# Four first column tiles woven together by halves of rows, and 512-column matmuls that take both halves of an activation in the last three projections

## The chip, the cores and the metric

One Trainium2 chip, one core of it. The metric is device microseconds (us) of one execution of the whole program. Engines are called PE (TensorE), DVE (VectorE), ACT (ScalarE), POOL (GpSimd) and SP (SyncE, which here only issues DMAs).

## The reference

One decoder layer over 16 learned meta tokens and 256 real tokens (T = 272 columns of work), width 2048. In short:

```
u     = rmsnorm(h, ln1_w)
p     = u @ w_in                       # one wide input projection for three mixers and three gates
o_h, o_m, o_r = hgrn2(p_h), mamba2(p_m), rwkv7(p_r)
mixed = g0 * (o_h @ w_up_h) + g1 * (o_m @ w_up_m) + g2 * (o_r @ w_up_r)
h     = h + mixed @ w_out
u     = rmsnorm(h, ln2_w)
h     = h + square(relu(u @ w_mlp_in)) @ w_mlp_out
return rmsnorm(h, lnf_w)               # the 256 real tokens
```

Everything is float32. The output projection is 2048 x 2048, the MLP 2048 x 8192 and 8192 x 2048.

## The kernel before

Tokens lie along the free axis and channels on the 128 partitions. Every projection is done one **column tile** at a time: 128 output channels, whose weights come as one or two **pieces** of 8 row blocks (128 x 1024 values, 512 KB each). `weights` (L210) has SP load a piece into `raw`, then calls `split` (L200): ACT rounds it to `wh` (fp32r, the high part), DVE subtracts and leaves the rest in `wl`. `raw`, `wh` and `wl` have three buffers each (`raw` gets three more after the output projection). Activations are split the same way, into `uh`/`ul` for the normed input, `mh`/`ml` for `mixed`, `zh`/`zl` for the second normed input and `hh`/`hl` for the hidden layer.

`product` (L228) then does three matmuls per row block into one of three PSUM buffers `pt`: high weights by high activations (L237), high weights by low activations (L238), low weights by high activations (L239). A full tile of 2048 rows is 16 row blocks, so 48 matmuls, each with its own weight load.

The program's stages are in this order: x is loaded and scaled (L276 to L285), its squares are summed on ACT, POOL, DVE and PE (L288 to L295), which gives `rstd1`; the RWKV tiles `wl`, `aldt`, `gl` 0 and `gl` 1 are projected one after the other (L365 to L375), each multiplied by `rstd1` in `proj` (L299); then come the other mixer tiles between the mixers' own small matmuls, the gates, and the three up-projections. Behind them stand the output projection (`out`, 16 tiles, L1161), and the MLP in four quarters: 16 tiles `mi` (2048 rows each, L1181) that fill a quarter of the hidden layer, then 16 tiles `mo` (L1190) that add it up in `macc`. The tail (L1205 to L1216) sums squares, takes the inverse root and scales the 16 output blocks on DVE and POOL, two blocks to a DMA.

Instructions are put in order for each engine by a scheduler that runs over the program with its own model of times; `tc.high_priority()` lets weight loads and splits go ahead. So the order on an engine isn't the order of the code, and a matmul that would wait for an activation can be put behind matmuls of the next tile.

Of the kernel before, what the change touches and what calls it, by code (L numbers as in the profile page):

```python
# [18 lines left out]
P = 128  # L19
D = 2048  # L20
# [130 lines left out]
def tile_hybrid(ctx: ExitStack, tc: tile.TileContext, a, out, dbg=None):  # L151
# [23 lines left out]
    def V(k, j=0, n=1, rows=slice(0, P)):  # L175
        return vecs[rows, VCOL[k] + j:VCOL[k] + j + n]
# [13 lines left out]
    def uname(s):  # L190
        cnt[0] += 1
        return f"{s}_{cnt[0]}"

    def trunk_psum(w):
        return ps_t.tile([P, 512], F32, tag="t", bufs=3, name=uname("pt"))[:, :w]

    def mx():
        return ps_x.tile([P, 512], F32, tag="x", bufs=5, name=uname("px"))

    def split(dst_h, dst_l, src):  # L200
        act.copy(dst_h, src)  # L201
        vec.tensor_tensor(dst_l, src, dst_h.bitcast(F32), sub)  # L202
# [69 lines left out]
    with ExitStack() as st:  # L272
        np_ = pool(st, "norm1", side="right")
        xt = np_.tile([P, KT, T], F32, name="xt")
        with tc.high_priority():
# [6 lines left out]
        for q in range(4):  # L282
            for kt in range(4 * q, 4 * q + 4):
                act.activation(uh[:, kt], xt[:, kt], AF.Copy, scale=V("ln1", kt))
                vec.scalar_tensor_tensor(ul[:, kt], xt[:, kt], V("ln1", kt),  # L285
                                         uh[:, kt].bitcast(F32), mult, sub)
        for q in range(4):
            x4 = xt[:, 4 * q:4 * q + 4]  # L288
            sq = np_.tile([P, 4, T], F32, tag="sq", bufs=2, name=uname("sq"))
            act.activation(sq[:, 0:2], x4[:, 0:2], AF.Square)  # L290
            nc.gpsimd.tensor_tensor(sq[:, 2:4], x4[:, 2:4], x4[:, 2:4], mult)
            nc.gpsimd.tensor_tensor(sq[:, 0:2], sq[:, 0:2], sq[:, 2:4], add)
            vec.tensor_tensor(sq[:, 0], sq[:, 0], sq[:, 1], add)
            pe.matmul(ssq, lhsT=C("ones"), rhs=sq[:, 0], start=(q == 0), stop=(q == 3))
        inv_sqrt(rstd1, ssq, 1.0 / D, eps_n)  # L295

    ALL, REAL = slice(0, T), slice(NM, T)

    def proj(key, tok=ALL, ahead=True):  # L299
        ps = product(key, uh, ul, tok, ahead=ahead)  # L300
        vec.tensor_tensor(ps, ps, rstd1[:, tok], mult)
        return ps


    omu = const.tile([P, 28], F32, name="omu")
    vec.tensor_scalar(omu, V("mu", 0, 28), -1.0, 1.0, mult, add)
    omka = const.tile([P, 8], F32, name="omka")
# [49 lines left out]
    REAL2 = slice(NM - 2, T)  # L357
# [6 lines left out]
    ps = proj("wl", ahead=False)  # L364
    shifted(ps, 24, twl[R96], R96)  # L365
    sigmoid(twl[R96], twl[R96], sign=2.0)
    vec.tensor_scalar(twl[R96], twl[R96], 2.0, -1.0, mult, add)
    ps = proj("aldt", ahead=False)
    shifted(ps, 25, alr[0:112], slice(0, 112))
    for j in range(2):  # L370
        ps = proj(("gl", j), REAL2)
        if j == 0:
            nc.sync.dma_start(cst, a["cst"])
        shifted(ps, 26 + j, sgl[:, j], skip=2)
        sigmoid(sgl[:, j], sgl[:, j])  # L375

    cr = {}
# [746 lines left out]
            nc.sync.dma_start(dbg[n], t)  # L1124
    st_x = ExitStack()
    xp = pool(st_x, "xp", side="right")
    mh = xp.tile([P, 16, NR], F32R, name="mh")
    ml = xp.tile([P, 16, NR], F32R, name="ml")
    hi, lo = branch_parts(o_h)
    for c in range(16):  # L1130
        up_next("uph", c, hi, lo, gate_back("gh", c))
        split(mh[:, c], ml[:, c], mixed[:, c])
    if "mixed" in dbg:
        nc.sync.dma_start(dbg["mixed"], mixed)
    st_g.close()
# [5 lines left out]
    ep = pool(st_e, "ep")  # L1141
    wp2 = pool(st_e, "wp2")
    h1 = ep.tile([P, 16, NR], F32, name="h1")
    zh = ep.tile([P, 16, NR], F32R, name="zh")
    zl = ep.tile([P, 16, NR], F32R, name="zl")
# [15 lines left out]
    for c in range(16):  # L1161
        xr = et("xr", 3)
        nc.scalar.dma_start(xr, a["xt"][:, c, NM:])
        ps = product(("out", c), mh, ml, RT)
        vec.tensor_tensor(h1[:, c], ps, xr, add)
        z = et("z")
        act.activation(z, h1[:, c], AF.Copy, scale=V("ln2", c))
        split(zh[:, c], zl[:, c], z)
        add_square(c, h1[:, c])
    more_raw.append((wp2, 3))  # L1170
    st_x.close()
# [5 lines left out]
    st_y = ExitStack()  # L1177
    yp = pool(st_y, "yp", side="right")
    for qd in range(4):
        hh = yp.tile([P, 16, NR], F32R, tag="hh", bufs=2, name=uname("hh"))  # L1180
        hl = yp.tile([P, 16, NR], F32R, tag="hl", bufs=2, name=uname("hl"))  # L1181
        for c in range(16):
            ps = product(("mi", 16 * qd + c), zh, zl, RT)
            r = et("rl")
            act.activation(r, ps, AF.Relu)
            s = et("rs")
            vec.tensor_tensor(s, r, r, mult)
            split(hh[:, c], hl[:, c], s)
# [21 lines left out]
    rf = et("rl")  # L1210
    inv_sqrt(rf, pn, 1.0 / D, eps_n)
    act.activation(h1[:, 15], h1[:, 15], AF.Copy, scale=V("lnf", 15))
    for c in range(16):
        (nc.gpsimd if c % 4 == 3 else vec).tensor_tensor(macc[:, c], h1[:, c], rf, mult)  # L1214
        if c % 2:
            (nc.sync if c % 4 == 1 else nc.scalar).dma_start(out[:, c - 1:c + 1], macc[:, c - 1:c + 1])  # L1216
    st_y.close()
    st_e.close()

# [95 lines left out]
```

## Time and profile before

| | |
|---|---|
| median of 3 runs | 1935.28 us (1934.91 to 1935.75) |
| the profiled execution, whole | 1936.93 us |
| its span, first to last instruction | 1935.1 us |
| PE busy | 1906.0 us of the span, 16220 matmuls |
| DVE, ACT, POOL busy | 1242.9, 1048.3, 185.5 us |
| HBM | 340 MB moved, 175 GB/s over the span |

The rows are those of one profiled execution. A matmul's listed time is from its start to the end of its result; a matmul starts long before the one ahead has ended, so the distance from one start to the next is what it costs, and the listed time is longer. The profile counts a plain float32 matmul as two (two passes), an fp32r matmul as one.

### The profile page before, as it was taken

To read this page: it belongs to the slowest core of one execution; us is meant where nothing else is said; L and a number is where in the kernel's file an instruction comes from. 1 tells how busy PE (TensorE), PEld (TensorE's weight loads), DVE (VectorE), ACT (ScalarE), POOL (GpSimd) and SP (SyncE) were. 2 spreads that over 40 slices of the span, in tenths; PEclk is the share of its full clock that TensorE was granted. 3 is DMA by queue.
4 is the path that set the end of the run, shared out by engine and by line. 5 is a ranking of instruction groups with operands and counts; after the bars stand their busy time and mean duration, and the time that the engine had idled before them with its cause. 6 is when DMAs were issued, how large, how long until landed. Compare 5 with 4: busy or idle time off the path is not lost.

```text
span 1935.1 us, 39773 instructions
## 1 busy us (share of the span) xinstructions
PE 1906.0 (98%) x16220; PEld 1866.0 (96%) x16220; DVE 1242.9 (64%) x1992; ACT 1048.3 (54%) x1857; POOL 185.5 (10%) x318
## 2 busy tenths in 40 slices
PE   6999999999999999999999999999999999999997
PEld 6999999999999999999999999999999999999997
DVE  7878676567956566777677765544455555665565
ACT  5666666566556667766564455444444344334453
POOL 4020111111111111112111000000000000000000
PEclk9999999999999999999999999999999999999999
DMA  5556544445554445445656776555555555555552
GB/s 211 183 179 202 164 150 135 146 154 158 175 174 147 145 144 193 144 150 168 200 168 213 247 218 190 182 184 185 185 186 185 186 183 181 185 185 183 185 185 99
DMA packets 104119, 340.39 MB, mean 176 GB/s; under 512 B 18216, under 2 KB 21432, under 8 KB 103936
## 3 DMA queue, kind: packets, MB, share of 16 engines
q1 hardware_dynamic: 91904, 315.25, 51.0%
q0 software_dynamic: 8576, 17.67, 3.0%
q10 hardware_dynamic: 3456, 4.93, 0.7%
q8 instruction: 127, 2.08, 0.5%
q14 instruction: 56, 0.46, 0.1%
HBM read 327.72 MB, written 10.08 MB: 175 GB/s over the span
## 4 chain that ended last, share of the span: by engine, by line
PE 97%; DVE 1%; DMA 0%; issue 0%; ACT 0%; SPq 0%; DVEq 0%; POOLq 0%
PE pt L239 29%; PE pt L237 29%; PE pt L238 29%; PE px L1025 1%; PE px L551 1%; PE px L657 0%; PE px L639 0%; PE px L694 0%; PE px L565 0%; PE px L559 0%; DVE macc L1214 0%; PE px L480 0%; PE px L623 0%; PE px L627 0%; PE px L661 0%; PE px L848 0%
## 5 line engine op out<-in xcount | busy, mean ns | idle before, releaser
L202 DVE TENSOR_TENSOR wl<-raw,wh 128x1024 fp32r<-128x1024 f32 x592 | 725.6, 1226 | 452.1 <-ACT wh L201 444.8
L201 ACT CAST wh<-raw 128x1024 fp32r<-128x1024 f32 x592 | 620.4, 1049 | 706.2 <-PE pt L238 491.1
L237 PE MATMUL pt<-uh,wh 128*128 128x256 f32 (+3 forms) x2048 | 587.6, 287 | 9.2 <-ACT wh L201 9.2
L239 PE MATMUL pt<-uh,wl 128*128 128x256 f32 (+3 forms) x2048 | 587.9, 287 | 4.0 <-DVE wl L202 4.0
L238 PE MATMUL pt<-ul,wh 128*128 128x256 f32 (+3 forms) x2048 | 587.6, 287 | 1.7 <-DVE ul L285 1.7
L237 PEld LDWEIGHTS pt<-uh,wh 128*128 128x128 f32 x2048 | 387.8, 189 | 12.6 <-ACT wh L201 9.2
L239 PEld LDWEIGHTS pt<-uh,wl 128*128 128x128 f32 x2048 | 387.7, 189 | 8.1 <-DVE wl L202 4.6
L238 PEld LDWEIGHTS pt<-ul,wh 128*128 128x128 f32 x2048 | 387.2, 189 | 6.3 <-DVE ul L285 2.6
L239 PE MATMUL pt<-zh,wl 128*128 128x256 f32 x1024 | 290.0, 283 | 0.0
L238 PE MATMUL pt<-zl,wh 128*128 128x256 f32 x1024 | 289.8, 283 | 0.0
L237 PE MATMUL pt<-zh,wh 128*128 128x256 f32 x1024 | 289.8, 283 | 0.0
L239 PE MATMUL pt<-hh,wl 128*128 128x256 f32 x1024 | 288.0, 281 | 0.0
L238 PE MATMUL pt<-hl,wh 128*128 128x256 f32 x1024 | 288.0, 281 | 0.0
L237 PE MATMUL pt<-hh,wh 128*128 128x256 f32 x1024 | 287.8, 281 | 0.0
L237 PEld LDWEIGHTS pt<-zh,wh 128*128 128x128 f32 x1024 | 196.6, 192 | 0.0
L239 PEld LDWEIGHTS pt<-zh,wl 128*128 128x128 f32 x1024 | 196.6, 192 | 0.0
L238 PEld LDWEIGHTS pt<-zl,wh 128*128 128x128 f32 x1024 | 196.6, 192 | 0.0
L237 PEld LDWEIGHTS pt<-hh,wh 128*128 128x128 f32 x1024 | 192.8, 188 | 0.0
L238 PEld LDWEIGHTS pt<-hl,wh 128*128 128x128 f32 x1024 | 192.7, 188 | 0.0
L239 PEld LDWEIGHTS pt<-hh,wl 128*128 128x128 f32 x1024 | 192.7, 188 | 0.0
L239 PE MATMUL pt<-oh,wl 128*128 128x256 f32 x384 | 108.3, 282 | 0.0
L237 PE MATMUL pt<-oh,wh 128*128 128x256 f32 x384 | 108.2, 282 | 0.0
(451 smaller groups left out, 2388.0 us busy)
## 6 DMA issues: line engine op xcount, KB each, us to landing
raw<-in_w SPq DMA_DIRECT2D x592, 512.0 KB, 3.5
rcb<-sc_rc SPq DMA_DIRECT2D x8, 256.0 KB, 4.1
sc_gr<-gt POOLq DMA_DIRECT2D x16, 128.0 KB, 3.7
sc_gm<-gt POOLq DMA_DIRECT2D x16, 128.0 KB, 3.6
sc_gh<-gt POOLq DMA_DIRECT2D x16, 128.0 KB, 3.7
gin<-sc_gr POOLq DMA_DIRECT2D x16, 128.0 KB, 3.0
gin<-sc_gm POOLq DMA_DIRECT2D x16, 128.0 KB, 3.1
gin<-sc_gh POOLq DMA_DIRECT2D x16, 128.0 KB, 3.4
```

The lines of the kernel that those rows point to most:

```text
L201: act.copy(dst_h, src)
L202: vec.tensor_tensor(dst_l, src, dst_h.bitcast(F32), sub)
L237: pe.matmul(ps, lhsT=wh[:, j], rhs=hi[:, kt, tok], start=(kt == 0), stop=False)
L238: pe.matmul(ps, lhsT=wh[:, j], rhs=lo[:, kt, tok], start=False, stop=False)
L239: pe.matmul(ps, lhsT=wl[:, j], rhs=hi[:, kt, tok], start=False, stop=(k == last and j == 7))
L551: pe.matmul(pk[e][:, c], lhsT=kt_[er, t], rhs=ar[er, :, t], start=True, stop=True)
L1025: pe.matmul(px[br, 2 * i + c], lhsT=xc, rhs=xc, start=True, stop=True)
```

## The change

At the start, all of x and the first three weight pieces are issued on SP's queue, in the order in which they are used. The tiles `wl`, `aldt`, `gl` 0 and `gl` 1 get a PSUM buffer each and are worked in two rounds: first the upper 8 row blocks of all four, then the lower 8. The splits of x (`x_parts`) stand between the splits of the first pieces. The squares and small preparations on DVE are told to come behind the last split of x, the sums of the squares go to POOL alone, and one matmul in place of four adds them over partitions.

In `out`, `mi` and `mo` the high and low activations lie in one tile (`m2`, `z2`, `hx`). `product2` does two matmuls per row block: high weights by 512 columns (both parts), whose results stand in the two halves of one PSUM bank, and low weights by the 256 high columns, added to the lower half. The two halves are added afterwards on DVE, where one of them must first be copied out by ACT (`low_part`) or goes through `h1` or `macc`.

In the tail the inverse root is written to PSUM and to SBUF; DVE scales 13 blocks in five instructions, POOL three, and six DMAs write the output.

```
+    def product2(key, x):
+        full = trunk_psum(2 * NR)
+        for k, (wh, wl) in enumerate(weights(key)):
+            for j in range(8):
+                kt = 8 * k + j
+                end = kt == KT - 1
+                pe.matmul(full.rearrange("p (a n) -> p a n", a=2), lhsT=wh[:, j], rhs=x[:, :, kt],
+                          start=(kt == 0), stop=end, skip_group_check=True)
+                pe.matmul(full[:, :NR], lhsT=wl[:, j], rhs=x[:, 0, kt], start=False, stop=end,
+                          skip_group_check=True)
+        return full[:, :NR], full[:, NR:]
...
+        FIRST = (("wl", ALL), ("aldt", ALL), (("gl", 0), REAL2), (("gl", 1), REAL2))
...
-            for q in range(4):
-                (nc.scalar if q else nc.sync).dma_start(xt[:, 4 * q:4 * q + 4],
-                                                        a["xt"][:, 4 * q:4 * q + 4])
+            load_x(0, 2)
+            raws = [raw_piece(FIRST[0][0], 0, 2)]
+            load_x(2, 4)
+            load_x(4, 8)
+            raws += [raw_piece(key, 0) for key, _ in FIRST[1:3]]
+            load_x(8, 12)
+            load_x(12, 16)
+        first = [mx()[:, :tok.stop - tok.start] for _, tok in FIRST]
...
+        for k in range(2):
+            for i, (key, tok) in enumerate(FIRST):
+                raw = raws.pop(0) if raws else raw_piece(key, k)
...
+                steps = 2 if k == 0 and i == 0 else 1
+                for m in range(steps):
+                    s = slice(8 // steps * m, 8 // steps * (m + 1))
+                    if steps == 2:
+                        x_parts(4 * m, 4 * m + 2)
+                    with tc.high_priority():
+                        split(wh[:, s], wl[:, s], raw[:, s])
+                    if steps == 2:
+                        x_parts(4 * m + 2, 4 * m + 4)
...
+                if k == 0 and i in (1, 2):
+                    x_parts(4 * i + 4, 4 * i + 8)
+        for q in range(8):
+            sq = np_.tile([P, 2, T], F32, tag="sq", bufs=2, name=uname("sq"))
+            with tc.issue_after(last_x[0]):
+                act.activation(sq if q else ssum, xt[:, 2 * q:2 * q + 2], AF.Square)
+            if q:
+                nc.gpsimd.tensor_tensor(ssum, ssum, sq, add)
+        nc.gpsimd.tensor_tensor(ssum[:, 0], ssum[:, 0], ssum[:, 1], add)
+        pe.matmul(ssq, lhsT=C("ones"), rhs=ssum[:, 0], start=True, stop=True)
...
+    def low_part(lo):
+        t = et("lo", 2)
+        act.copy(t, lo)
+        return t
...
-        ps = product(("out", c), mh, ml, RT)
-        vec.tensor_tensor(h1[:, c], ps, xr, add)
+        ps, lo = product2(("out", c), m2)
+        vec.tensor_tensor(h1[:, c], lo, xr, add)
+        vec.tensor_tensor(h1[:, c], ps, h1[:, c], add)
...
-            ps = product(("mi", 16 * qd + c), zh, zl, RT)
+            ps, lo = product2(("mi", 16 * qd + c), z2)
+            vec.tensor_tensor(ps, ps, low_part(lo), add)
             r = et("rl")
             act.activation(r, ps, AF.Relu)
...
-            ps = product(("mo", qd, c), hh, hl, RT)
+            ps, lo = product2(("mo", qd, c), hx)
...
+            if qd < 3:
+                vec.tensor_tensor(macc[:, c], lo, macc[:, c], add)
+            else:
+                vec.tensor_tensor(ps, ps, low_part(lo), add)
...
+    act.activation(rl, pn, AF.Ln, bias=eps_n, scale=1.0 / D)
+    act.activation(rp_, rl, AF.Exp, scale=-0.5)
+    act.activation(rf, rl, AF.Exp, scale=-0.5)
+    for k, (lo, hi) in enumerate(((0, 2), (2, 5), (5, 8), (8, 11), (11, 13))):
+        vec.tensor_tensor(macc[:, lo:hi], h1[:, lo:hi],
+                          rp_.unsqueeze(1).to_broadcast([P, hi - lo, NR]), mult)
+        (nc.scalar if k % 2 else nc.sync).dma_start(out[:, lo:hi], macc[:, lo:hi])
+    for c in range(13, 16):
+        nc.gpsimd.tensor_tensor(macc[:, c], h1[:, c], rf, mult)
+    nc.scalar.dma_start(out[:, 13:16], macc[:, 13:16])
```

Two places show how the scheduler's order moves. The first is **DVE at the start**. `ul` is the low part of x, `wl_...` that of a weight piece, `lbt`, `omu` and the like are small preparations. Before, from the seventh row:

```order
L285 SCALAR_TENSOR_TENSOR ul<-xt,vecs,uh 128x272 x4
L320 RECIPROCAL lbt<-lbt 128x8
L321 TENSOR_TENSOR lbt<-lbt 128x8
L322 TENSOR_TENSOR lbt<-lbt 128x8
L323 TENSOR_SCALAR lbt<-lbt 128x8
L202 TENSOR_TENSOR wl_192<-raw_189,wh_191 128x1024
L285 SCALAR_TENSOR_TENSOR ul<-xt,vecs,uh 128x272 x3
```

And now, from the first:

```order
L325 SCALAR_TENSOR_TENSOR ul<-xt,vecs,uh 128x272 x2
L202 TENSOR_TENSOR wl_112<-raw_96,wh_111 128x512 x2
L325 SCALAR_TENSOR_TENSOR ul<-xt,vecs,uh 128x272 x6
L202 TENSOR_TENSOR wl_158<-raw_101,wh_157 128x1024
L202 TENSOR_TENSOR wl_194<-raw_103,wh_193 128x1024
L325 SCALAR_TENSOR_TENSOR ul<-xt,vecs,uh 128x272 x8
L379 TENSOR_SCALAR omu<-vecs 128x28
```

The small preparations have moved behind the sixteen splits of x, and the first piece is split in two halves after two blocks of x.

The second is **PE where a quarter goes from `mi` to `mo`**, at the last row block of the first `mo` tile, which needs the hidden block that was finished last. Before, that tile is `pt_16232`, the next one `pt_16294`:

```order
L237 MATMUL pt_16294<-hh_15158,wh_16297 128x256
L238 MATMUL pt_16232<-hl_15159,wh_16241 128x256
L239 MATMUL pt_16232<-hh_15158,wl_16242 128x256
L238 MATMUL pt_16294<-hl_15159,wh_16297 128x256
L239 MATMUL pt_16294<-hh_15158,wl_16298 128x256
L237 MATMUL pt_16294<-hh_15158,wh_16303 128x256
L238 MATMUL pt_16294<-hl_15159,wh_16303 128x256
```

And now, where that tile is `pt_15787`, the next one `pt_15834` and the one after it `pt_15881`:

```order
L251 MATMUL pt_15834<-hx_14922,wh_15843 128x512
L251 MATMUL pt_15787<-hx_14922,wh_15796 128x512
L253 MATMUL pt_15787<-hx_14922,wl_15797 128x256
L253 MATMUL pt_15834<-hx_14922,wl_15844 128x256
...
L253 MATMUL pt_15834<-hx_14922,wl_15844 128x256
L251 MATMUL pt_15881<-hx_14922,wh_15884 128x512
L253 MATMUL pt_15881<-hx_14922,wl_15885 128x256
```

Before, 26 matmuls of the next tile follow on the pair that was put off, and that next tile still has its whole second piece ahead; now five follow, and then the third tile begins, whose first piece takes over the buffers `wh` and `wl` which that pair read last. The same five stand at all four such places.

## Rows read from the trace of the kernel before

**Rows 1.** The page: busy time of each engine with its share and instructions, and the chain that ended last.
```profile
PE 1906.0 (98%) x16220; PEld 1866.0 (96%) x16220; DVE 1242.9 (64%) x1992; ACT 1048.3 (54%) x1857; POOL 185.5 (10%) x318
PE 97%; DVE 1%; DMA 0%; issue 0%; ACT 0%; SPq 0%; DVEq 0%; POOLq 0%
```

**Rows 2.** Stretches: busy us (x instructions) of PE, PEld, DVE, ACT, POOL; PEclk, DMA share, GB/s.
```profile
40.00:1000.00 960.00, 958.89 (x8312) 922.90 (x8312) 673.08 (x1228) 604.88 (x1229) 140.33 (x232) 1.00 0.52 164
1300.00:1500.00 200.00, 200.00 (x1679) 200.00 (x1679) 98.88 (x108) 86.06 (x115) 0.00 (x0) 1.00 0.58 185
```

**Rows 3.** What PE waited for over the whole span: us in total, times, longest.
```profile
PE pt L237 <- ACT wh L201: 9.2, 1, 9.2
PE pt L239 <- DVE wl L202: 4.0, 2, 2.4
PE pt L238 <- DVE ul L285: 1.7, 3, 0.9
```

**Rows 4.** Timeline of the first 25 us: start, us, engine, line, op, xcount [idle before <-releaser].
```profile
5.44 1.76 ACT L284 ACTIVATE uh<-xt,vecs 128x272 fp32r<-128x272 f32 x4 [3.42 <-DMA vecs<-in_vecs]
7.11 0.64 ACT L290 ACTIVATE sq<-xt 128x544 f32<-128x544 f32 x1
9.19 0.59 PE L237 MATMUL pt<-uh,wh 128*128 128x272 f32 x1 [9.19 <-ACT wh L201]
11.13 1.22 DVE L202 TENSOR_TENSOR wl<-raw,wh 128x1024 fp32r<-128x1024 f32 x1
12.41 0.59 PE L239 MATMUL pt<-uh,wl 128*128 128x272 f32 x1 [2.41 <-DVE wl L202]
17.54 4.07 DVE L285 SCALAR_TENSOR_TENSOR ul<-xt,vecs,uh 128x272 fp32r<-128x272 f32 x3
21.53 2.36 DVE L202 TENSOR_TENSOR wl<-raw,wh 128x1024 fp32r<-128x1024 f32 x1
```

**Rows 5.** Stretches near the start, columns as in rows 2.
```profile
5.00:6.00 1.00, 0.00 (x0) 0.00 (x0) 0.62 (x1) 0.56 (x2) 0.75 (x1) 1.00 1.06 435
24.00:28.00 4.00, 4.00 (x18) 4.00 (x19) 2.68 (x5) 0.00 (x0) 3.87 (x14) 0.50 0.62 186
```

**Rows 6.** The tile xt, first 30 us: x count, ns min/median/max of one, first and last start.
```profile
L285 DVE SCALAR_TENSOR_TENSOR ul<-xt,vecs,uh x16: 489/494/1593, 6.8 to 25.1; 128x272 fp32r<-128x272 f32 x16
```

**Rows 7.** The chain that ended last, in order of time: start, us, what.
```profile
63.85 0.46 PE px L432 x2
```

**Rows 8.** Groups by line and shape: x count, busy us, mean ns of one.
```profile
L207 PE MATMUL px<-sqh,onesr 128*128 128x512 f32 x4 | 1.6, 402 | 0.0
L208 PE MATMUL px<-sql,onesr 128*128 128x512 f32 x4 | 1.6, 394 | 0.0
L237 PE MATMUL pt<-oh,wh 128*128 128x256 f32 x384 | 108.2, 282 | 0.0
```

**Rows 9.** Timeline of PE at two 512-column matmuls.
```profile
814.34 0.41 PE L207 MATMUL px<-sqh,onesr 128*128 128x512 f32 x1
814.58 0.49 PE L977 MATMUL px<-cst,iv 128*128 128x128 f32 x3
...
1032.34 0.28 PE L237 MATMUL pt<-oh,wh 128*128 128x256 f32 x1
1032.45 0.40 PE L207 MATMUL px<-sqh,onesr 128*128 128x512 f32 x1
1032.69 0.28 PE L238 MATMUL pt<-ol,wh 128*128 128x256 f32 x1
```

**Rows 10.** Timeline of ACT and DVE at the first change from mi to mo.
```profile
1282.73 1.05 ACT L201 CAST wh<-raw 128x1024 fp32r<-128x1024 f32 x1 [1.52 <-issue]
1283.82 1.22 DVE L202 TENSOR_TENSOR wl<-raw,wh 128x1024 fp32r<-128x1024 f32 x1 [1.29 <-ACT wh L201]
```

**Rows 11.** Timeline of the tail.
```profile
1920.98 0.42 DVE L1200 TENSOR_TENSOR rs<-pt,r 128x256 f32<-128x256 f32 x1 [3.90 <-PE pt L239]
1924.06 6.22 DVE L1214 TENSOR_TENSOR macc<-h,rl 128x256 f32<-128x256 f32 x12 [2.19 <-ACT rl L252]
```

More of the change, by code (lines that the diff above doesn't have):

```diff
@@ L258, in tile_hybrid @@
     eps_n, eps_g = eps[:, 0:1], eps[:, 1:2]
+    ALL, REAL = slice(0, T), slice(NM, T)
+    REAL2 = slice(NM - 2, T)
     st_o = ExitStack()
@@ L274, in tile_hybrid, with raw_piece, load_x @@
         xt = np_.tile([P, KT, T], F32, name="xt")
+        FIRST = (("wl", ALL), ("aldt", ALL), (("gl", 0), REAL2), (("gl", 1), REAL2))
+        def raw_piece(key, k, parts=1):
+            raw = wp.tile([P, 8, P], F32, tag="raw", bufs=3, name=uname("raw"))
+            src = a["w"][PIECE[key][0] + k].rearrange("p (j m) -> p j m", j=8)
+            for i in range(parts):
+                s = slice(8 // parts * i, 8 // parts * (i + 1))
+                nc.sync.dma_start(raw[:, s], src[:, s])
+            return raw
+        def load_x(lo, hi):
+            nc.sync.dma_start(xt[:, lo:hi], a["xt"][:, lo:hi])
         with tc.high_priority():
@@ L287, in tile_hybrid @@
[L287 to L294, printed above, removed]
+            load_x(0, 2)
@@ new lines, in tile_hybrid, with x_parts @@
+            raws = [raw_piece(FIRST[0][0], 0, 2)]
[5 more added lines that the diff above has]
+        first = [mx()[:, :tok.stop - tok.start] for _, tok in FIRST]
+        last_x = []
+        def x_parts(lo, hi):
+            with tc.high_priority():
+                for kt in range(lo, hi):
+                    ia = act.activation(uh[:, kt], xt[:, kt], AF.Copy, scale=V("ln1", kt))
+                    iv = vec.scalar_tensor_tensor(ul[:, kt], xt[:, kt], V("ln1", kt),
+                                                  uh[:, kt].bitcast(F32), mult, sub)
+            if hi == KT:
+                last_x.extend((ia.ins, iv.ins))
@@ new lines, in tile_hybrid @@
+        for k in range(2):
+            for i, (key, tok) in enumerate(FIRST):
+                raw = raws.pop(0) if raws else raw_piece(key, k)
+                wh = wp.tile([P, 8, P], F32R, tag="wh", bufs=3, name=uname("wh"))
+                wl = wp.tile([P, 8, P], F32R, tag="wl", bufs=3, name=uname("wl"))
+                steps = 2 if k == 0 and i == 0 else 1
[3 more added lines that the diff above has]
+                        x_parts(4 * m, 4 * m + 2)
+                    with tc.high_priority():
+                        split(wh[:, s], wl[:, s], raw[:, s])
+                    if steps == 2:
+                        x_parts(4 * m + 2, 4 * m + 4)
+                    for j in range(s.start, s.stop):
+                        kt = 8 * k + j
+                        pe.matmul(first[i], lhsT=wh[:, j], rhs=uh[:, kt, tok], start=(kt == 0),
+                                  stop=False)
+                        pe.matmul(first[i], lhsT=wh[:, j], rhs=ul[:, kt, tok], start=False,
+                                  stop=False)
+                        pe.matmul(first[i], lhsT=wl[:, j], rhs=uh[:, kt, tok], start=False,
+                                  stop=(kt == KT - 1))
+                if k == 0 and i in (1, 2):
+                    x_parts(4 * i + 4, 4 * i + 8)
@@ new lines, in tile_hybrid @@
+        ssum = np_.tile([P, 2, T], F32, name="ssum")
+        for q in range(8):
[5 more added lines that the diff above has]
+        nc.gpsimd.tensor_tensor(ssum[:, 0], ssum[:, 0], ssum[:, 1], add)
+        ssq = mx()[:, :T]
+        pe.matmul(ssq, lhsT=C("ones"), rhs=ssum[:, 0], start=True, stop=True)
@@ L295, in tile_hybrid @@
         inv_sqrt(rstd1, ssq, 1.0 / D, eps_n)
-    ALL, REAL = slice(0, T), slice(NM, T)
+        for ps, (_, tok) in zip(first, FIRST):
+            vec.tensor_tensor(ps, ps, rstd1[:, tok], mult)
     def proj(key, tok=ALL, ahead=True):
@@ L302, in proj @@
         return ps
+    late = ExitStack()
+    for ins in last_x:
+        late.enter_context(tc.issue_after(ins))
     omu = const.tile([P, 28], F32, name="omu")
@@ L362, in tile_hybrid @@
     R96 = slice(0, 96)
-    ps = proj("wl", ahead=False)
-    shifted(ps, 24, twl[R96], R96)
+    shifted(first[0], 24, twl[R96], R96)
     sigmoid(twl[R96], twl[R96], sign=2.0)
     vec.tensor_scalar(twl[R96], twl[R96], 2.0, -1.0, mult, add)
-    ps = proj("aldt", ahead=False)
-    shifted(ps, 25, alr[0:112], slice(0, 112))
+    shifted(first[1], 25, alr[0:112], slice(0, 112))
     for j in range(2):
-        ps = proj(("gl", j), REAL2)
         if j == 0:
             nc.sync.dma_start(cst, a["cst"])
-        shifted(ps, 26 + j, sgl[:, j], skip=2)
+        shifted(first[2 + j], 26 + j, sgl[:, j], skip=2)
         sigmoid(sgl[:, j], sgl[:, j])
@@ L1126, in tile_hybrid @@
     xp = pool(st_x, "xp", side="right")
-    mh = xp.tile([P, 16, NR], F32R, name="mh")
-    ml = xp.tile([P, 16, NR], F32R, name="ml")
+    m2 = xp.tile([P, 2, 16, NR], F32R, name="m2")
     hi, lo = branch_parts(o_h)
@@ L1143, in tile_hybrid @@
     h1 = ep.tile([P, 16, NR], F32, name="h1")
-    zh = ep.tile([P, 16, NR], F32R, name="zh")
-    zl = ep.tile([P, 16, NR], F32R, name="zl")
+    z2 = ep.tile([P, 2, 16, NR], F32R, name="z2")
     acc2 = ep.tile([P, NR], F32, name="acc2")
@@ L1209, in tile_hybrid @@
     pe.matmul(pn, lhsT=C("ones"), rhs=s, start=False, stop=True)
-    rf = et("rl")
-    inv_sqrt(rf, pn, 1.0 / D, eps_n)
     act.activation(h1[:, 15], h1[:, 15], AF.Copy, scale=V("lnf", 15))
[L1213 to L1216, printed above, removed]
+    rl, rf = et("rl"), et("rs")
+    rp_ = mx()[:, :NR]
+    act.activation(rl, pn, AF.Ln, bias=eps_n, scale=1.0 / D)
[8 more added lines that the diff above has]
+    nc.scalar.dma_start(out[:, 13:16], macc[:, 13:16])
     st_y.close()
```

16 lines of the change are left out of this document (5 added, 11 removed).

## The prediction

> **What bounds the kernel now.** I read the page first: PE is busy for 1906.0 of 1935.1 us, and the chain that ended last is PE for 97% [rows 1]. DVE and ACT stand at 64% and 54% and lie beside it. So time is won only where PE has less to do, or where PE stands still. Two stretches show its pace: from 1300 to 1500 us, in the MLP, PE runs 1679 matmuls in 200 us without a gap, 119.1 ns each; from 40 to 1000 us it stands for 1.1 of 960 us, so whatever the start wins is handed on through the mixers [rows 2]. The list of PE's waits says where it stands: 9.2 us for the first `wh`, 4.0 for `wl`, 1.7 for `ul`, all in the first 25 us [rows 3]. The rest is the tail, some 14 us after the last trunk matmul [rows 11].
>
> **The price of a 512-column matmul.** The change takes one matmul and one weight load from each row block of `out`, `mi` and `mo`: 16 + 64 + 64 tiles of 16 blocks, 2304 in all. The columns streamed stay the same (256 three times, or 512 and 256), so only what a matmul costs beside its columns is saved. The kernel already has eight fp32r matmuls of 512 columns, in the sums of `L207` and `L208`. They are listed with 402 and 394 ns, a 256-column matmul of the trunk beside them with 282 [rows 8]: 112 to 120 ns more, 116 in the mean. With a step of 119.1 that makes 235 ns for 512 columns, and the timeline agrees: 0.24 us from start to start at 1032.45 [rows 9]. Two matmuls of 256 take 238.2. The saving is 3.1 ns for a row block, times 2304 = **7.1 us**.
>
> The bounds: if 512 columns cost just two times 256, nothing. If all that a 256-column matmul costs over its columns at 2.4 GHz (119.1 - 106.7 = 12.4 ns) were saved, 28.6 us. Below nothing: see the last rival. I take 3.1 because it is read off the same kind of matmul among the same neighbours.
>
> The Trainium skill (TensorE: Matmul & The Clock Gate, "LDWEIGHTS (loading the stationary operand)") gives a weight load as its columns divided by 1.2 in ns, so an estimate of 107 ns for 128 columns, about as long as 256 columns of streaming. By it the 119 ns would be loads and matmuls getting in each other's way, and the 512 columns would hide their load: that is the first rival below.
>
> **What is added to the other engines.** For each tile of `mi` ACT copies `lo` out of PSUM and DVE adds, some 0.4 us each by the small DVE row of the tail [rows 11]; `out` and `mo` get one DVE addition more, in the last quarter also the copy. Beside PE's 5.6 us for a tile, DVE has about half of its time free (98.9 us busy of 200) and ACT more [rows 2]. These cost nothing while `pt` comes free in time, and it has three buffers, two tiles or 11 us ahead. The weight stream stays at about 185 GB/s with a DMA share of 0.58, where 435 GB/s were moved at the start [rows 2, 5].
>
> **Where a quarter goes from `mi` to `mo` (four times).** The last block of the first `mo` tile is put off until its `hx` is there, which I reckon some 6.5 us after the last `mi` matmul, while the pair stands 10 us behind it; that wait costs nothing. But the pair holds the buffers of `wh` and `wl` that the third tile's first piece must take, and only five matmuls (three of 256, two of 512) follow on the pair before that tile begins. From the start of the pair's first matmul: it ends after 0.40 us, the rounding takes 1.05 [rows 8, 10], with hand-overs `wh` is there at 1.6; PE has run out of work at 0.235 + 0.119 + 0.83 = 1.18. Then `wl` takes 1.22 more [rows 10] and is there at 2.85, while PE's first matmul of the tile lets it get to 1.84. So it stands 0.4 and 1.0 us, 1.4 at each change, **+5.8 us** in all. Before, 26 matmuls (3.1 us) plus the next tile's second piece lay there, and no such wait is in the list. Bounds: 0, if splits overlap better than I reckon, and 8.
>
> **The start.** Up to the first `L432` at 63.85 us [rows 7] PE has the same 336 trunk matmuls before and after: 192 of 272 columns, which I take at 126 ns (119 and 16 columns more), and 144 of 256 to 258 at 119, together 41.3 us, and the sums of squares. The other 20 us are lost to waits and to the clock: from 24 to 28 us it was granted at 0.50, 1.2 GHz, after PE had stood for most of four microseconds, and 18 matmuls took 4.0 us, 222 ns each [rows 5].
>
> Now. The DMAs run at about 0.4 MB/us once they are going [rows 5]; by 13 us x (2.2 MB) and three pieces are in, in the order of use. I reckon x's first two blocks and `vecs` at about 4.2 us; a block of x costs ACT 0.44 us (four in 1.76) and DVE 0.49 [rows 4, 6], half a piece 0.5 and 0.65. PE then starts at about 5.8 us instead of 9.19, works through the first half tile at the pace of the splits, to 10.6, and waits for `wl` of the second piece until 12.0. The next two half tiles (44 matmuls, some of them at 1.2 GHz) end at 18.7.
>
> Then comes a gap. The splits of x end on ACT at 15.3 and on DVE at 16.3; ACT does three squares of 0.64 us [rows 4] before it casts the fourth piece, so that DVE can begin its `wl` at about 18.3. POOL is then adding squares, and beside such POOL work DVE's subtractions took 1.36 us instead of 0.49 and a `wl` 2.36 instead of 1.22 [rows 4, 6]. So that `wl` is there at 20.6, and PE has stood for about 1.5 us. From there DVE keeps ahead: five half tiles more, four of them 22 to 24 matmuls after a head start, to 34.8. One matmul of squares in two passes (0.46, as `L432` [rows 7]) and the 144 of the next three tiles (17.8 us) give 53.1, against 63.85: 10.7 us. I take off 0.7 for a second stretch at half clock that may follow on the gap: **-10 us**. Bounds: 7, if such a stretch comes as long as the one before; 13, if POOL doesn't slow DVE.
>
> The sums of squares come later, but `rstd1` is wanted only by DVE and ACT for tiles whose `pt` are free for 18 us. SP now issues all of x and passes nothing that is needed sooner; `cst` goes behind x, and the fourth piece behind `cst`, which I reckon at 16 us, before ACT gets to it.
>
> **The tail.** The copy of `lo` and one addition lengthen the chain by 0.8 us. The scaling was twelve DVE instructions in 6.22 us, slowed by POOL [rows 11]; now 13 blocks go in five, two of 512 and three of 768 columns, which at 1.22 us for 1024 [rows 10] are 4.0 us, 4.0 to 5.6 with POOL beside. Together **-0.7 us** (bounds -1.4 and +0.2).
>
> **The sum.** -7.1 + 5.8 - 10 - 0.7 = -12.0 us. On the profiled execution (1936.9, its span 1935.1 and 1.8 around it) that is 1924.9; the median of the runs lies 1.65 lower, so 1923.3: **1923 us**.
>
> **The rivals.** Differences under 0.2% (3.9 us: faster below 1931.4, slower above 1939.2) are what a measurement of this kernel can't tell from none.
>
> 1. *The fixed part goes whole.* If the 119 ns come from loads that a 512-column matmul hides, 12.4 ns go for each block: 28.6 us instead of 7.1, **1902 us**. For it: PEld is listed busy without a gap in the MLP [rows 2]. Against: the 512-column matmul of rows 9 had all that time for the next load and still took 0.24 us.
> 2. *Nothing is saved on columns.* 512 cost as two of 256, and the waits at the four changes stay: 1923 + 7 = **1930 us**. The upper end of 120 ns in rows 8 is this case.
> 3. *The start stays bound by the splits.* If POOL and DVE block each other for longer, and PE's clock falls again while it waits, the first four tiles win only some 3 us: **1930 us**. For it: DVE needs 8 us for x and 10 for eight pieces, and stood in PE's way before [rows 3]. Against: before, that happened with the same work in a worse order.
> 4. *Slower: the two segments of the moving operand cost.* The 512 columns of `x[:, :, kt]` lie in two rows 16 KB apart; no row shows such a matmul. At 0.244 us, as at 814.34 before plain float32 matmuls [rows 9], the block takes 363 instead of 357.3 ns, 13 us more: 1935.3 - 10 + 5.8 - 0.7 + 13 = **1943 us**. It decides from about 242 ns on; below that the start makes up for it.
>
> **How the numbers follow.** Forecast 0.50, first rival 0.15, second 0.14, third 0.12, fourth 0.09. The forecast and the first rival are faster; the second and third lie 1 us from the line, I give each half to faster and half to the same; the fourth is slower by two parts in three, else the same. Faster 0.78, same 0.16, slower 0.06. The range goes from the first rival's 1903 to 1931, which leaves out the fourth and the far ends of the others.
>
> **What would show it.** In the new profile: some 2304 matmuls fewer; a step of about 0.235 us after a matmul of `hx` or `z2` with 512 columns and 0.119 after one of 256; in PE's waits four on `wl` and four on `wh` after the changes from `mi` to `mo`, 1.4 us together at each; the first matmul near 5.8 us, and the first matmul by `lora` near 53 us. The prediction is wrong in its main term if a row block of the MLP takes less than 350 or more than 358 ns, and wrong in the start if that matmul lies outside 50 to 57 us.

## The result, and the profile after

The changed kernel took **1914.41 us** (median of 4 runs, 1914.12 to 1915.05) against 1935.1 us (1934.74 to 1935.75) for the kernel before on the same chip: a ratio of 0.9893, with a 95% interval from 0.9876 to 0.991. The forecast was 1923 us, the range 1903 to 1931. The time lies in the range and on the side that was given 0.78, but 8.6 us below the number: the sum held 12 of the some 21 us that were won. Its terms show why.

The page of the changed kernel, its busy times and its chain [rows 1]:

```profile
span 1912.6 us, 35367 instructions
PE 1890.1 (99%) x13910; PEld 1747.1 (91%) x13910; DVE 1289.5 (67%) x2126; ACT 1074.5 (56%) x1943; POOL 187.5 (10%) x317
PE 98%; DVE 1%; DMA 0%; ACT 0%; issue 0%; SPq 0%; DVEq 0%
```

PE has 2310 matmul records fewer: 2304 in `out`, `mi` and `mo`, and 6 because the squares of the start are added by one plain float32 matmul (two records) in place of four. PE's own busy time fell by 15.9 us and the span by 22.5, so the other 6.6 us are time in which PE no longer stands. DVE got 134 instructions and 46.6 us more, and the chain still goes through PE for 98%: the work added to DVE and ACT lies beside PE, as the forecast had it.

Where PE stood, from the list of its waits [rows 3]:

```profile
PE px L346 <- ACT wh L201: 8.4, 2, 6.2
PE px L1285 <- ACT sqe L1284: 1.9, 1, 1.9
PE px L346 <- ACT uh L324: 1.2, 1, 1.2
```

The waits for `wh`, `wl` and `ul` of the start came to 14.9 us and are now 9.6: 6.2 before the first matmul, 2.2 at a gap at 20 us, 1.2 for x. The eight waits expected at the changes from `mi` to `mo` are not there. `L1285` is the tail.

Stretches [rows 2, 5]; columns are the stretch, its length, busy us (x instructions) of PE, PEld, DVE, ACT, POOL, then PEclk, DMA share, GB/s:

```profile
10.00:14.00 4.00, 4.00 (x19) 4.00 (x19) 3.27 (x7) 3.66 (x7) 0.00 (x0) 1.00 1.02 418
24.00:28.00 4.00, 4.00 (x35) 4.00 (x34) 3.78 (x4) 2.01 (x4) 3.84 (x3) 1.00 0.88 277
40.00:1000.00 960.00, 959.97 (x8349) 923.39 (x8349) 679.42 (x1248) 610.12 (x1246) 147.24 (x245) 1.00 0.51 164
895.00:1898.00 1003.00, 1003.00 (x6292) 896.66 (x6291) 647.82 (x938) 496.42 (x763) 32.58 (x54) 1.00 0.58 189
1300.00:1500.00 200.00, 200.00 (x1138) 174.39 (x1138) 114.16 (x149) 91.29 (x130) 0.00 (x0) 1.00 0.57 187
```

From 24 to 28 us the clock is granted in full in this execution, and PE does 35 matmuls where it did 18 at 0.50 [rows 5]. From 895 to 1898 us, which holds all of `out`, `mi` and `mo`, PE never stands. In the MLP PEld, busy without a gap before [rows 2], now has 25.6 of 200 us free.

The price of a row block (all its matmuls, from its first start to that of the next block) is read over a whole quarter, `mi` and `mo`, 32 tiles of 16 blocks, from the first `mi` matmul of one quarter to that of the next. On PE's timeline (start, length) of the kernel before:

```profile
1370.90 0.28 PE L237 MATMUL pt<-zh,wh 128*128 128x256 f32 x1
...
1554.19 0.28 PE L237 MATMUL pt<-zh,wh 128*128 128x256 f32 x1
```

and of the changed one, with a few blocks in between:

```profile
1357.54 0.40 PE L251 MATMUL pt<-z,wh 128*128 128x512 f32 x1
...
1399.94 0.40 PE L251 MATMUL pt<-z,wh 128*128 128x512 f32 x1
1400.18 0.28 PE L253 MATMUL pt<-z,wl 128*128 128x256 f32 x1
1400.29 0.40 PE L251 MATMUL pt<-z,wh 128*128 128x512 f32 x1
...
1537.88 0.39 PE L251 MATMUL pt<-z,wh 128*128 128x512 f32 x1
```

183.29 us before and 180.34 after, over 512 blocks: 358.0 and 352.2 ns, **5.8 ns saved for a block**. From start to start a 512-column matmul takes 0.23 to 0.24 us, in the mean of the stretch from 1300 to 1500 us 233.1 ns, and a 256-column one 119.0.

Where the 22.5 us of the span went, on the starts of single matmuls in the two traces (before to after): the first `lora` matmul, which ends the start, 63.69 to 55.63, **-8.1**; the first matmul of `out` 1096.05 to 1086.94, another **-1.1**; the last trunk matmul 1920.66 to 1898.40, another **-13.1**; from there to the end 14.5 to 14.2, **-0.3**. The profiled execution before lay 1.8 us above its median, the one after on it, so the medians differ by 20.7. The 1.1 us answer to a row in the list of waits of the kernel before that is gone from the list of the new one:

```profile
PE px L607 <- DMA xb<-sc_x: 1.0, 1, 1.0
```

### The profile page after: what moved, and what is told of

It reads as the page before. It is cut to its first block, busy times and chain, and to the rows that moved or that the text cites. A ratio compares the mean times of both kernels' runs of the same rounds, so it can differ in the third digit from the quotient of the medians.

```text
span 1912.6 us, 35367 instructions
## 1 busy us (share of the span) xinstructions
PE 1890.1 (99%) x13910; PEld 1747.1 (91%) x13910; DVE 1289.5 (67%) x2126; ACT 1074.5 (56%) x1943; POOL 187.5 (10%) x317
## 4 chain that ended last, share of the span: by engine, by line
PE 98%; DVE 1%; DMA 0%; ACT 0%; issue 0%; SPq 0%; DVEq 0%
PE pt L251 28%; PE pt L239 15%; PE pt L237 15%; PE pt L238 15%; PE pt L253 14%; PE px L1093 1%; PE px L619 1%; DMA xt<-in_xt 0%; PE px L725 0%; PE px L707 0%; PE px L633 0%; PE px L762 0%; PE px L627 0%; PE px L548 0%; PE px L346 0%; PE px L691 0%
## 5 line engine op out<-in xcount | busy, mean ns | idle before, releaser
L202 DVE TENSOR_TENSOR wl<-raw,wh 128x1024 fp32r<-128x1024 f32 (+1 forms) x593 | 726.4, 1225 | 397.3 <-ACT wh L201 389.4
L201 ACT CAST wh<-raw 128x1024 fp32r<-128x1024 f32 (+1 forms) x593 | 621.9, 1049 | 652.8 <-PE pt L238 239.1
L237 PE MATMUL pt<-uh,wh 128*128 128x256 f32 (+2 forms) x1984 | 567.9, 286 | 0.0
L238 PE MATMUL pt<-ul,wh 128*128 128x256 f32 (+2 forms) x1984 | 567.0, 286 | 0.0
L251 PE MATMUL pt<-z,wh 128*128 128x512 f32 x1024 | 362.2, 399 | 0.0
L251 PE MATMUL pt<-hx,wh 128*128 128x512 f32 x1024 | 358.9, 393 | 0.0
L253 PE MATMUL pt<-hx,wl 128*128 128x256 f32 x1024 | 287.9, 283 | 0.0
L253 PE MATMUL pt<-z,wl 128*128 128x256 f32 x1024 | 287.4, 281 | 0.0
L253 PEld LDWEIGHTS pt<-z,wl 128*128 128x128 f32 x1024 | 193.4, 189 | 0.1
L253 PEld LDWEIGHTS pt<-hx,wl 128*128 128x128 f32 x1024 | 192.5, 188 | 0.9
```

The source lines that it names most:

```text
L251: pe.matmul(full.rearrange("p (a n) -> p a n", a=2), lhsT=wh[:, j], rhs=x[:, :, kt], start=(kt == 0), stop=end, skip_group_check=True)
L253: pe.matmul(full[:, :NR], lhsT=wl[:, j], rhs=x[:, 0, kt], start=False, stop=end, skip_group_check=True)
```

## The experiments

The theory after the result: two parts that don't touch each other, a start that is some 9 us shorter and 2304 blocks that are 5.8 ns cheaper each, and no wait at the four changes. The rivals: one part brings its gain only together with the other; the saving on blocks is not the merged matmul; the gap at 20 us is bound by something else than `lbt`.

**Each part alone.** The first kernel is the one before with only the hunks of the start, the second the one before with only `product2` in `out`, `mi` and `mo`:

```diff
+        for k in range(2):
+            for i, (key, tok) in enumerate(FIRST):
+                raw = raws.pop(0) if raws else raw_piece(key, k)
...
         ps = product(("out", c), mh, ml, RT)
```

> The new start alone, on the old output projection, MLP and tail. In the two traces the first matmul by lora moved from 63.7 to 55.6 us (8.1 us), and another 1.1 us went at the 1.19 us pause of L607 near 221 us. If start and MLP add up: 1935.1 - 9.1 = 1926 us. Rival: part of the start's gain shows only because the MLP is shorter (a shared bound such as the weight stream): then less than 5 us, over 1930 us.

Measured: 1927.49 us, ratio 0.9958 (0.9943 to 0.9973), 8.4 us less than before on that chip.

```diff
             for kt in range(4 * q, 4 * q + 4):
                 act.activation(uh[:, kt], xt[:, kt], AF.Copy, scale=V("ln1", kt))
...
-        ps = product(("out", c), mh, ml, RT)
+        ps, lo = product2(("out", c), m2)
```

> The old start and tail, only product2 in the output projection and the MLP. The stretch from the first out tile to the last mo tile took 13.2 us less in the changed kernel. If this belongs to the 2304 removed matmuls alone: 1935.1 - 13.2 = 1922 us. Rival: if the MLP's gain needs the earlier start, 1928 us or more.

Measured: 1922.84 us, ratio 0.9934 (0.9918 to 0.9951), 13.0 us less. The list of PE's waits has the old start again, and nothing at the changes:

```profile
PE pt L237 <- ACT wh L201: 9.1, 1, 9.1
PE pt L239 <- DVE wl L202: 4.1, 2, 2.4
PE px L1231 <- ACT sqe L1230: 1.9, 1, 1.9
PE pt L238 <- DVE ul L299: 0.9, 2, 0.6
PE px L621 <- DMA xb<-sc_x: 0.7, 1, 0.7
```

8.4 and 13.0 make 21.4, and the whole change brought 20.7: the parts add up. The traces say it more sharply. From the first matmul of `out` to the last trunk matmul it takes 824.61 us before and 811.46 after; 824.61 with the new start alone, and 811.46 with `product2` alone. The wait at `L607` is gone with the new start alone, and 0.7 of it stays with the old one.

**Three matmuls again.** Everything of the change, but the 512-column matmul in two:

```diff
-                pe.matmul(full.rearrange("p (a n) -> p a n", a=2), lhsT=wh[:, j], rhs=x[:, :, kt],
+                pe.matmul(full[:, :NR], lhsT=wh[:, j], rhs=x[:, 0, kt],
                           start=(kt == 0), stop=end, skip_group_check=True)
+                pe.matmul(full[:, NR:], lhsT=wh[:, j], rhs=x[:, 1, kt],
+                          start=False, stop=end, skip_group_check=True)
```

> The changed kernel with the 512-column matmul of product2 split in two of 256, high and low part: as many matmuls and weight loads as before the change, all else (one tile for both parts, two halves of the bank, additions, order rules) as in the changed kernel. If the gain is what a matmul costs beside its columns (5.7 ns for each of 2304): 1914.4 + 13.2 = 1927.6 us. Rival: the gain comes from the layout or from waits that went: then 1914 to 1918 us.

Measured: 1928.6 us, ratio 0.9961 (0.9946 to 0.9976), 14.2 us above the change, or 6.2 ns for each of 2304 blocks. Its trace is back at 358.0 ns for a block, and at 824.62 us from the first matmul of `out` to the last trunk matmul. So the saving is the merged matmul, and not the separate sum of the low part, the tail or the order. In 200 us of the MLP PE is back at the count of before [rows 2], with PEld full again:

```profile
1300.00:1500.00 200.00, 200.00 (x1679) 200.00 (x1678) 110.92 (x145) 90.57 (x130) 0.00 (x0) 1.00 0.56 185
```

**What still holds the block at 352 ns.** Fewer columns in the matmul of the low weights, first 224, then 192, tell what a column is worth there (both kernels leave out a part of the product, the low weights of the last 32 or 64 tokens):

```diff
-                pe.matmul(full[:, :NR], lhsT=wl[:, j], rhs=x[:, 0, kt], start=False, stop=end,
+                pe.matmul(full[:, :224], lhsT=wl[:, j], rhs=x[:, 0, kt, :224], start=False, stop=end,
```

> The changed kernel, but the matmul of the low weights takes 224 columns in place of 256; the part of the low weights for the last 32 tokens is left out. It asks what sets the 119 ns of a 256-column matmul beside a 512-column one. If columns do (about 0.43 ns each beyond a fixed part): 14 ns less for each of 2304, 1914.4 - 32 = 1882 us. If a weight load is a floor, as the 111 ns of 128-column plain float32 matmuls suggest: 8 ns less, 1896 us. If the load alone sets 119 ns: no change, 1914 us.

Measured: 1895.11 us, ratio 0.9789 (0.9774 to 0.9803). That is 19.3 us less than the change, 8.4 ns for a block (343.3 ns in the trace, 8.9 less), where 32 columns at 2.4 GHz are 13.3.

> As the run with 224 columns, but with 192 in the matmul of the low weights: it leaves out the low-weight part of the last 64 tokens. At 224 columns a row block took 343.4 ns where 352.1 less 32 columns (13.3 ns) would be 338.8, and the weight load after it looked like the limit. Load theory: the load of the high weights can't hide behind fewer columns, the sum of a block stays near 343, 1895 us (1890 to 1898). Column theory (the 4.6 ns missing at 224 were something else that happens once): 13.3 ns less for each of 2304 blocks again, 31 us, 1865 us.

Measured: 1897.06 us, ratio 0.98 (0.9784 to 0.9816). The second 32 columns bring nothing: the intervals of the two ratios overlap, and a block takes 344.8 ns in the trace. PE's timeline with 224 columns:

```profile
1400.64 0.40 PE L251 MATMUL pt<-z,wh 128*128 128x512 f32 x1
1400.88 0.26 PE L253 MATMUL pt<-z,wl 128*128 128x224 f32 x1
1400.98 0.40 PE L251 MATMUL pt<-z,wh 128*128 128x512 f32 x1
```

and with 192:

```profile
1400.24 0.42 PE L251 MATMUL pt<-z,wh 128*128 128x512 f32 x1
1400.50 0.25 PE L253 MATMUL pt<-z,wl 128*128 128x192 f32 x1
1400.59 0.42 PE L251 MATMUL pt<-z,wh 128*128 128x512 f32 x1
```

Together with that short matmul starts the load of the next high weights, and 0.11 us behind it the load of the next low ones:

```profile
1400.50 0.19 PEld L251 LDWEIGHTS pt<-z,wh 128*128 128x128 f32 x1
1400.61 0.19 PEld L253 LDWEIGHTS pt<-z,wl 128*128 128x128 f32 x1
```

A block takes 0.34 to 0.35 us in both: the start after the 512-column matmul comes later by what the short one gives up (0.24 and 0.10, then 0.26 and 0.09). So the sum of the two steps stops at some 343 to 345 ns, and columns are not what stops it. The weight loads are what stays: from the load of the high weights to the next load it is 119.2 ns in the changed kernel from 1300 to 1500 us, as long as the 256-column step, and 109.1 ns in the mean with 224 columns and with 192 alike. That a load takes about this long, and sets the distance where the matmul is shorter, fits; no run took the loads away without the matmuls, so it is not shown beyond that.

**The gap at 20 us.** On ACT's timeline of the changed kernel:

```profile
17.86 1.19 ACT L359 ACTIVATE sq<-xt 128x544 f32<-128x544 f32 x2
18.96 1.04 ACT L201 CAST wh<-raw 128x1024 fp32r<-128x1024 f32 x1
21.59 0.21 ACT L392 ACTIVATE lbt<-lbt 128x8 f32<-128x8 f32 x1 [1.59 <-DVE lbt L391]
21.70 1.03 ACT L201 CAST wh<-raw 128x1024 fp32r<-128x1024 f32 x1
```

The cast that PE needs at 20.4 us, the second one shown, stands behind one step of 128x8, which waits for DVE. And on DVE and POOL:

```profile
18.80 1.35 DVE L385 TENSOR_SCALAR nwa<-vecs 128x16 f32<-128x16 f32 x1
20.26 1.30 DVE L391 TENSOR_TENSOR lbt<-vecs,lbt 128x8 f32<-128x8 f32 x1
...
18.76 2.77 POOL L361 TENSOR_TENSOR ssum<-ssum,sq 128x544 f32<-128x544 f32 x2
```

Two DVE steps take 1.35 and 1.30 us while POOL's two additions run. In the kernel before, the same two took 0.16 and 0.17:

```profile
6.44 0.16 DVE L312 TENSOR_SCALAR nwa<-vecs 128x16 f32<-128x16 f32 x1
6.70 0.17 DVE L318 TENSOR_TENSOR lbt<-vecs,lbt 128x8 f32<-128x8 f32 x1
```

They also stand before DVE's `wl` of the fourth piece, whose cast was done at 20.0 us and which ran from 21.48 to 22.69. So PE, which went on at 22.78, lacked two things at once; the edit frees both and doesn't part them. It moves the preparation of `lbt`, which is first read after 700 us, behind the last of the first four tiles:

```diff
-    lbt = const.tile([P, 6, 8], F32, name="lbt")
...
-    vec.tensor_scalar(lbt[:, 5], lbt[:, 4], -1.0, 1.0, mult, add)
...
+    after_sgl = ExitStack()
+    after_sgl.enter_context(tc.issue_after(sgl_done))
+    lbt = const.tile([P, 6, 8], F32, name="lbt")
...
+    vec.tensor_scalar(lbt[:, 5], lbt[:, 4], -1.0, 1.0, mult, add)
...
+    after_sgl.close()
```

> The changed kernel with the preparation of lbt (a chain of small DVE steps with one ACT step, first used by the HGRN2 part) put behind the last of the four first tiles. In the changed kernel PE pauses from 20.3 to 22.8 us for a wh whose rounding stands on ACT behind that step. If the chain is the cause: the pause goes but for what the wl needs, 1.5 to 2.5 us less, 1912 to 1913 us. Rival: the piece or the rounding comes late for another reason (squares on ACT, the load): no change, 1914.4 us.

Measured: 1912.48 us, ratio 0.9881 (0.9865 to 0.9898), 1.9 us below the change.

> The version with the late lbt chain once more, on the same chip as the other two, as their reference: 1912.5 us (1911.5 to 1913.5) by every theory.

Measured: 1912.3 us, ratio 0.9878 (0.9865 to 0.9891). PE's longest wait in this run:

```profile
PE px L346 <- ACT wh L201: 6.6, 2, 6.1
```

The wait at the gap fell from 2.2 us to 0.5, and the chain has its first `lora` row at 53.48 us in the first of the two runs and at 54.00 in the second, where it stood at 55.80. The intervals of the ratios overlap with the change's, so the timing alone wouldn't decide it; the traces do. In the six that have the new start with `lbt` unmoved (the change and five of the runs here) PE stands for 2.1 to 2.3 us at this gap, and the first `lora` matmul starts at 54.3 to 56.8 us; in the five with `lbt` moved it stands for 0.45 at most, and `lora` starts at 53.2 to 54.0. This is the **fastest complete version of the study**.

The spread among the six has a cause that the trace of the change hides. In four of them (the new start alone, three matmuls, 224 columns, the wide gates) the granted clock fell to 0.50 for a time behind the gap; here with three matmuls:

```profile
24.00:28.00 4.00, 4.00 (x24) 4.00 (x24) 3.40 (x4) 1.08 (x2) 3.84 (x3) 0.64 0.84 263
```

From the end of the gap to `lora` those four take 34.3 to 34.4 us, the other two 32.8 to 32.9: 1.5 us more. None of the five with `lbt` moved has such a stretch in its start.

**The same form in the input projections.** 72 tiles of the input projection (the gates, `z`, `q`, `g`) use 256 columns three times too. With `product2` there, ACT copies the low part and DVE adds it, as in `mi`:

```diff
-    uh = upool.tile([P, KT, T], F32R, name="uh")
-    ul = upool.tile([P, KT, T], F32R, name="ul")
+    u2 = upool.tile([P, 2, KT, T], F32R, name="u2")
+    uh, ul = u2[:, 0], u2[:, 1]
...
+            ps, lo = product2(key, u2, tok)
+            act.copy(tmp, lo)
+            vec.tensor_tensor(ps, ps, tmp, add)
```

> The changed kernel with 512-column matmuls also in the 72 input tiles of 256 columns (gates, z, q, g): 1152 row blocks more, each with a copy on ACT and an addition on DVE more. If a removed matmul gives 5.7 ns everywhere and the additions stay hidden: 6.6 us less, 1908 us. Rival: between the mixers DVE is busy for 70 to 80% and its additions come onto PE's path, or the scheduler's order gets worse: no gain or a loss, 1914 us and more.

Measured: 1925.95 us, ratio 0.9947 (0.9932 to 0.9962), 11.5 us slower than the change. With the late `lbt` as well:

> Both edits together (late lbt, 512 columns in the 72 input tiles). If they add up: 1906 us; if the second doesn't gain: 1912 us and more.

Measured: 1921.79 us, ratio 0.9926 (0.9911 to 0.9941), 9.3 us slower than without the wide tiles. To see where, the tiles were parted, each kind on the version with the late `lbt`:

> The version with the late lbt chain, and the 512-column form also in the 16 tiles of q and g (256 row blocks), not in the 56 of the gates and z. Theory: the loss of the wider version sits at three waits between the mixers before 500 us and in the stretch at half clock behind them; q and g lie later, beside free engines, so they win what a row block of the MLP won: 256 x 5.8 ns = 1.5 us, 1911.0 us (1910 to 1912). Rival: every widened tile costs by its extra copy and addition, so a share of 16/72 of the 9.3 us lost there: 1914.6 us.

Measured: 1913.07 us, ratio 0.9883 (0.9869 to 0.9896).

> The complement: the late lbt chain, the 512-column form in the 56 tiles of the gates and z, not in q and g. Theory: the three waits and the half clock are all here, 1921.8 + 1.5 = 1923 us, with the waits at about 397, 478 and 491 us in the list of PE's waits. Rival (a loss shared by all widened tiles): 1912.5 + 9.3 x 56/72 = 1919.7 us.

Measured: 1921.15 us, ratio 0.9926 (0.9912 to 0.9939). The loss is in the gates and `z`. New in the list of PE's waits:

```profile
PE pt L251 <- ACT gt L259: 3.3, 1, 3.3
PE px L573 <- DVE tkb L568: 3.0, 1, 3.0
PE px L664 <- ACT xvm L657: 2.0, 1, 2.0
```

and the stretch of this run that holds them (columns as above):

```profile
300.00:500.00 200.00, 191.72 (x1333) 167.76 (x1332) 137.29 (x284) 123.61 (x265) 26.46 (x50) 0.98 0.43 143
```

Three waits of 8.3 us together, and a mean clock of 0.98 over 200 us (the trace has 6.8 us at the lower level in it, which cost 3.4), where the changed kernel loses 0.03 of 960 us from 40 to 1000 us, at 1.00. That is 11.7 of the 14 us by which the run misses the gain that 56 tiles x 16 blocks x 5.8 ns (5.2 us) would have given on 1912.3. All three waits are for ACT or DVE, between the mixers' short matmuls. Whether the cheaper tiles left these engines too little time, their extra copies and additions held them up, or the new order did, no run parts. Why `q` and `g` alone brought nothing, 0.8 us more instead of 1.5 less with intervals that overlap, stays open: their list of waits shows no new one above 0.2 us.

## Why the prediction was right, and where it wasn't

Each term of the sum, as forecast, and as the two traces have it: 512 columns -7.1, measured -13.1 (with the changes); the changes +5.8, measured 0; the start -10, measured -8.1 and 1.1 more at `L607`; the tail -0.7, measured -0.3. The forecast's own signs held: a block of 352.2 ns lies within 350 to 358, and `lora` at 55.6 us within 50 to 57. But the shares came out the other way round: the start was to bring 10 of 12 us and `out`, `mi` and `mo` 1.3; they brought 13.1 of 22.5. That the time still fell into the range owes much to the range, which reaches down to the first rival's time (given as 1903 there, as 1902 in the rival).

- **The price of a block was right in kind and too small in size**: 3.1 ns forecast, 5.8 measured over a quarter, 6.2 by taking the merge back. The step of 512 columns came out at 233.1 ns instead of 235, and the three matmuls had cost 358.0 and not 3 x 119.1 = 357.3. The mean of rows 2 is a count of records in 200 us; the distance between two starts, a quarter apart, would have given 358.0 ahead of time. A difference of 3 ns between numbers near 350 was read from rows good to 2 or 3.
- **The step that failed is the wait at the four changes.** It supposed that the third tile's first piece must take the buffers of the pair that is put off. On ACT's timeline of the first change in the new kernel:

```profile
1275.85 1.05 ACT L201 CAST wh<-raw 128x1024 fp32r<-128x1024 f32 x1 [2.18 <-PE pt L251]
1278.14 1.05 ACT L201 CAST wh<-raw 128x1024 fp32r<-128x1024 f32 x1 [1.25 <-PE pt L251]
```

  The pair that was put off runs at 1277.7 us, and the third tile begins 1.2 us behind it. The cast for that tile's first piece, the next in the order of use, began at 1275.85, released by a matmul: it took the buffer that the second tile's first piece had just left, not that of the pair. Only the piece after it (1278.14) waited for the pair, and it has half a tile of PE's work, 2.8 us, in front of it. The stretch from 895 to 1898 us agrees. I had read a rotation into the three buffers of `wh` which the order of the casts doesn't have.
- **The start** was forecast step by step and missed by 2.5 us, 2.2 of them before 23 us: the first matmul at 6.2 for 5.8, and the gap's end at 22.8 for 20.6. From there to `lora` it took 32.9 us, forecast 32.5. The step that failed is that after ACT's three squares and the cast of the fourth piece "DVE can begin its `wl` at about 18.3". The splits of x ended two microseconds later than forecast (17.4 on ACT, 18.6 on DVE, for 15.3 and 16.3), and then the small preparations came first, which the change moves behind the last block of x (the `late` lines of its diff): the `wl` began at 21.48 and was there at 22.69. In the kernel before they stood between 5 and 11 us, and were not free there either: on DVE's timeline `L321` and `L322` stand from 8.67 to 11.02, beside additions of POOL, right before the first `wl` (its cast was done at 9.13), for which PE waited 2.4 us [rows 4]. I had not counted what they would pass. Moving `lbt` away brought 1.9 us back, and `lora` came at 53.2 to 54.0, where 53.1 was forecast. The second stretch at half clock, put at 0.7 us, did not come in the profiled execution of the change; it came in four of the six with this start and cost 1.5, so -8.1 is the number of one execution, and a good one. The old start varies too: `lora` starts at 63.69 in the trace before and at 62.48 with `product2` alone.
- **The 1.1 us at `L607`** were not in the sum. They are the 1.1 of 960 us that PE stood in the mixers before [rows 2]; I took that pause as fixed; it is gone in the run with the new start alone, and 0.7 of it stays in the run with the old one.
- **The tail.** The scaling took 3.88 us, forecast 4.0 to 5.6, for 6.22 [rows 11], and begins 0.84 us later, as forecast. On DVE's timeline:

```profile
1902.64 3.88 DVE L1294 TENSOR_TENSOR macc<-h,px 128x512 f32<-128x512 f32 x5 [2.16 <-ACT px L1291]
```

  But 6.1 us lie from its end to the end of the span, 4.8 before: the outputs go out in 256 to 384 KB at a time, 2.9 to 3.5 us from issue to landing, where 256 KB took 2.2 to 2.5. That gave back 1.3 of the 1.5 us that the scaling had won, a price the forecast left out.
- **The rivals.** The first (the fixed part goes whole, 1902 us) fits in part on the mechanism and is too large in size: the loads of weights are no longer busy without a gap, but a block saved 5.8 of its 12.4 ns, nearer to the 3.1 forecast. The runs with 224 and 192 columns stop at a distance of 109.1 ns from the load beside the short matmul to the next. The Trainium skill (TensorE: Matmul & The Clock Gate, "LDWEIGHTS (loading the stationary operand)") gives a load as its columns divided by 1.2 in ns, an estimate of 107 ns for 128 columns; the 109.1 ns agree with it, and 224 or 192 columns stream in 93 or 80 ns at 2.4 GHz, too short to cover it. The second and the fourth rival are excluded (352.2 ns, not 358 or 363; two rows 16 KB apart cost the moving operand nothing that shows). The third is not borne out: the start won 8.1 us.

So the two savings are in the two places where the forecast put them, which is the part of the mechanism that was right; their sizes were not, with two errors of opposite sign in the order of work (5.8 us too dark at the changes, 2 too bright at the gap) and one in size (6 us).

## What to carry to other kernels

Where three matmuls share two stationary operands, merging the two that share one saved some 6 ns for each block here (two of 256 columns into one of 512); measure the step from starts far apart, since means over records hide that much. When a step is moved in a list, look at the smallest instructions that move with it: a few steps of 128x8, in the way of a cast and a split, cost 2 us of PE. And look at what lies between the tiles: the same edit lost 9 us where short matmuls that wait for two other engines did. Read the first microseconds from more than one execution.

## What was not expected of the hardware

- **A matmul shorter than a weight load didn't pay.** Beside a load of 128 columns for every matmul, 256 to 224 columns saved 8.9 ns for a block (352.2 to 343.3), and 224 to 192 nothing (344.8).
- **DVE stands for POOL's whole instruction.** `L385` began 0.04 us after the first of POOL's two additions (18.76 to 20.13 us) and ended at 20.15; `L391` began 0.06 after the second (20.20 to 21.53) and ended at 21.56. Without POOL beside them the same two steps took 0.16 and 0.17 us. The Trainium skill (SBUF — State Buffer, "Who interferes with whom") says that whoever issues first holds the shared ports for the whole instruction; these rows agree.
- **The first matmuls run at the pace of the lower clock, though the rows print 1.00.** On PE's timeline:

```profile
12.62 0.43 PE L346 MATMUL px<-uh,wh 128*128 128x272 f32 x1
12.85 0.43 PE L348 MATMUL px<-ul,wh 128*128 128x272 f32 x1
...
14.66 0.28 PE L350 MATMUL px<-uh,wl 128*128 128x272 f32 x1
14.78 0.29 PE L346 MATMUL px<-uh,wh 128*128 128x272 f32 x1
```

  0.226 us apart until 14.2 us, which is 272 columns at 1.2 GHz, and 0.126 from then on, after PE had worked without a listed wait since 9.4 us. The row from 10 to 14 us above prints 1.00 with only 19 matmuls. That is no reading: the trace has no record of the granted clock before 14.38 us, when full clock is granted, and a stretch without a record is printed as 1.00. The 19 cost 1.9 us that the start still holds.
